# First norm's two chains in turn, the last stores on two queues, and C's transposes at later steps, in a two-layer hybrid trunk

## The chip, the cores and the metric

The kernel runs on one core of one Trainium2 chip. The metric is the device time of one execution in microseconds (us). Before the change the median of three runs is 414.24 us (413.98 to 414.63). All durations below come from one profiled execution of that kernel, which took 414.05 us.

## What is computed

The input x has 256 tokens of 1024 numbers. Two layers are applied, each h = h + Mixer(RMSNorm(h)), and a last RMSNorm. Layer 0 is a sparse attention mixer (compressed, selected and window branches, 16 heads, gated), layer 1 a diagonal state-space mixer (S5). The parts that matter here:

```python
def _rmsnorm(x, g):
    return x * rsqrt(mean(x * x, -1) + EPS) * g

# S5 parameters, from weights alone
dt  = exp(log_dt);  lre = minimum(lambda_re, -1e-4)
mag = exp(lre * dt); ab = mag * (cos(lim * dt), sin(lim * dt))
coef = (ab - 1) / lambda
bb  = coef * b                 # complex, 64 groups x 64 states x 16
y   = Re(c * scan(ab, bb * u)) + d_skip * u
```

The state-space layer's matrices (`ep` from C and the powers of ab, `bbn` from b and the powers) depend on weights alone, so they are computed in the background while the attention layer runs.

## The kernel before, in words

All work is on one core: 256 tokens are two halves of 128 (j = 0, 1), the 1024 model columns are eight slices of 128 (k). Weights stream from memory through four buffers `raw`, loaded by SyncE (SP, L193). A planner orders each engine's instructions by simulated times and by their order in the program; inside `tc.manual_schedule(engines=...)` the named engines keep the order of the program.

**The first norm (L326 to L352).** Each half of x (`xin`) is transposed by TensorE (L338) into PSUM banks `bts`. ScalarE squares a half and sums it on the way (L336), first half 0, then half 1. From each sum VectorE computes a reciprocal square root in one column per partition: `rsqrt_steps` (L283 to L302) is a start value and three rounds of two steps (L287, L290, then L297 and L299 three times). Six steps of the first chain run ahead, then the chains alternate (L340 to L343). `row_bcast` (L310) writes a diagonal matrix on VectorE into a piece of `xn`, and a matmul with ones makes `rb`, the factors as rows. After copies to `g0c` and `rrow`, eight operations (L350) write `xn`, the normed and transposed x. ScalarE then issues the loads of b and C (`s5_loads`, L175).

**What follows on TensorE.** `PRE` (L28) lists the first projections: `v0`, then `v1` with L875 ahead of it (the transpose of `rows`, a tile of small weights that SyncE loads at L355 to L362), `k0`, `k1`, `gt` (gates), `ck`, `cv`, `q0`. `v0` and `v1` run at L280, the others at L267. Each takes a PSUM bank of two that rotate; the gates take the bank of `k0` and so wait until VectorE has written `kl` (L795) from it. A matmul with f32 operands stands as two records in the trace.

**The parameter chain.** `chain_gen` (L394 to L480) is the computation of dt, mag, coef and ab on VectorE, some 100 small operations, which end in `nat2`. It is traced at L642 with a low priority, so the planner puts its steps into VectorE's gaps, also into those of the first norm.

**The background generator.** `s5_gen` (L484 to L640) does the rest in steps divided by `yield`. `adv(n)` takes n steps; hooks take one step (from `v1` on) or two (from `k1` on) with each weight tile of `PRE`, and the main loop over 24 attention units takes three a unit (`PACE`, L1132). The step numbers: 1 copies of b, 2 and 3 the transposes of `nat2` (L493) and VectorE's copies of them (L494), 3 to 6 the powers `pw` (L377), 7 to 9 the products for b (L534 to L538), 10 and 11 the transposes of C (L541 to L550), 12 to 14 the products for b2 (L551 to L555), then 24 `ep` products (L571 to L575) and 48 `bbn` products with their transposes (L597 to L604). All products are on GpSimd (POOL, L383). A transposed half of C goes through the one PSUM bank of the background to `c1c` and `c2c`, by ScalarE (L546, L548):

```python
for q in range(2):
    bt2 = bg_bank()
    for t in range(4):
        T.transpose(bt2[:, t * P:(t + 1) * P], cnat[:, 4 * q + t]..., ident)
    ...
    yield
```

**The bias of the compressed branch.** GpSimd writes `cbias` at the start of the program's attention part, with four operations (L672 twice, L675 twice).

**The end (L1447 to L1510).** The last projection gives five pieces of the output; for each VectorE adds the residual (L1451), ScalarE squares and sums (L1452), and GpSimd multiplies with the norm's weights (L1455, not for piece 4). `finish(j, i)` computes the factor of a half and scales: half 0 on ScalarE (L1461), then four stores on SyncE (L1463); half 1 on ScalarE (columns 0 to 511, L1465) and VectorE (768 to 1023 at L1466, 512 to 767 at L1467), then four stores of the left half on SyncE (L1469) and four of the right half, on ScalarE's queue and SyncE in turn (L1471).

Of the kernel before, what the change touches and what calls it, by code (L numbers as in the profile page):

```python
# [8 lines left out]
F32 = mybir.dt.float32  # L9
# [7 lines left out]
P = 128  # L17
# [29 lines left out]
def kernel(  # L47
# [132 lines left out]

    hooks = []
# [143 lines left out]

    xn = actp.tile([P, KT, S], F32, tag="actT", name="xn")  # L326
    sqs = xn.rearrange("p (j k) s -> p j (k s)", j=NQ)
    bts = [bank().rearrange("p (k s) -> p k s", k=2) for _ in range(KT // 2)]
    rb, gb0 = bank(), bank()
    rrow = const.tile([P, S], F32, name="rrow")  # L330
    E_ = mybir.EngineType
    with tc.manual_schedule(engines={E_.DVE, E_.Pool, E_.Activation}):
        sums, ys = [], [[], []]
        for j in range(NQ):
            sums.append(smp.tile([P, 1], F32, tag="ss", name="ss"))
            A.activation(sqs[:, j], xin[:, j], AF.Square, accum_out=sums[j])  # L336
            for k in range(KT):
                T.transpose(bts[k // 2][:, k % 2, j * P:(j + 1) * P], xin[:, j, k * P:(k + 1) * P], ident)  # L338
        rq = [rsqrt_steps(sums[j], ys[j]) for j in range(NQ)]
        for _ in range(6):  # L340
            next(rq[0])
        for r in (rq[1], rq[0]) * 12:
            next(r, None)  # L343
        for j in range(NQ):
            row_bcast(*ys[j], rb[:, j * P:(j + 1) * P], sqs[:, j, 0:P])
        T.transpose(gb0[:, :KT], nrow, ident[:KT, :KT])
        V.tensor_copy(g0c, gb0[:, :KT])
        V.tensor_copy(rrow, rb[:, :S])
        for k in range(KT):
            V.scalar_tensor_tensor(xn[:, k], bts[k // 2][:, k % 2], g0c[:, k:k + 1], rrow,  # L350
                                   op0=ALU.mult, op1=ALU.mult)
        s5_loads()  # L352

    rows = const.tile([56, P], F32, name="rows")
    nc.sync.dma_start(rows[8:24], pe_k.rearrange("(k l) d -> k (l d)", l=2))  # L355
    nc.sync.dma_start(rows[24:40], pe_v.rearrange("(k l) d -> k (l d)", l=2))
    nc.sync.dma_start(rows[0:8], n1.rearrange("(k p) -> k p", p=P))
# [3 lines left out]
    for u in range(2):  # L361
        nc.sync.dma_start(r4[:, u], d4[1 - u])  # L362
# [279 lines left out]
    with tc.high_priority(-CHOFF):  # L642
        for _ in chain_gen():
            pass
# [895 lines left out]
```

## Time and profile before

| | us |
|---|---|
| median of three runs | 414.24 (413.98 to 414.63) |
| the profiled execution | 414.05 |
| its span, first to last instruction | 412.3 |
| TensorE (PE) busy | 354.2 (86%) |
| GpSimd (POOL) busy | 269.3 (65%) |
| VectorE (DVE) busy | 227.9 (55%) |
| ScalarE (ACT) busy | 178.4 (43%) |
| bytes moved | 52.03 MB, mean 126 GB/s |

The execution's time is 1.75 us longer than its span. A busy TensorE is not TensorE at its peak: its matmuls are pipelined, and its granted clock has two levels, shown as 1.00 (2.4 GHz) and 0.50 (1.2 GHz). The mean granted clock of the execution is 0.933. Idle time of an engine costs something only where the chain of waits passes through it.

### The profile page before, as it was taken

To read this page: it belongs to the slowest core of one execution; us is meant where nothing else is said; L and a number is where in the kernel's file an instruction comes from. 1 tells how busy PE (TensorE), PEld (TensorE's weight loads), DVE (VectorE), ACT (ScalarE), POOL (GpSimd) and SP (SyncE) were. 2 spreads that over 40 slices of the span, in tenths; PEclk is the share of its full clock that TensorE was granted. 3 is DMA by queue.
4 is the path that set the end of the run, shared out by engine and by line. 5 is a ranking of instruction groups with operands and counts; after the bars stand their busy time and mean duration, and the time that the engine had idled before them with its cause. 6 is when DMAs were issued, how large, how long until landed. Compare 5 with 4: busy or idle time off the path is not lost.

```text
span 412.3 us, 6834 instructions
## 1 busy us (share of the span) xinstructions
PE 354.2 (86%) x2505; PEld 293.0 (71%) x2505; DVE 227.9 (55%) x582; ACT 178.4 (43%) x397; POOL 269.3 (65%) x281
## 2 busy tenths in 40 slices
PE   3899599999999998968998879994858599999990
PEld 3688468865888787644766657783847599999890
DVE  4969904433355243524555498563999944264243
ACT  3212420145366467566784454342513335444432
POOL 7009459989987789999544489321872476665760
PEclk9699979999999999985999999998696899999996
DMA  8964315558633315411311335996741215655403
GB/s 256 158 172 114 110 53 153 152 190 244 181 103 99 106 57 178 126 52 51 103 36 58 113 103 99 172 87 180 251 156 54 71 34 158 199 163 200 152 2 102
DMA packets 59970, 52.03 MB, mean 126 GB/s; under 512 B 21928, under 2 KB 52704, under 8 KB 59872
## 3 DMA queue, kind: packets, MB, share of 16 engines
q1 hardware_dynamic: 49536, 50.41, 43.9%
q10 hardware_dynamic: 10400, 1.18, 2.2%
q8 instruction: 20, 0.33, 0.4%
q14 instruction: 14, 0.11, 0.1%
HBM read 48.17 MB, written 1.05 MB: 119 GB/s over the span
## 4 chain that ended last, share of the span: by engine, by line
PE 57%; DVE 16%; SPq 6%; POOL 6%; DMA 5%; issue 5%; ACT 3%; DVEq 0%; ACTq 0%; POOLq 0%
PE b L267 16%; SPq L1181 5%; PE b L280 4%; PE b L224 4%; PE b L225 4%; PE b L226 4%; PE ob L986 3%; PE tu L973 2%; PE b L246 2%; PE b L244 2%; PE b L245 2%; DVE pw L377 2%; POOL wl L209 2%; PE cm L745 2%; DVE bbT L1357 2%
## 5 line engine op out<-in xcount | busy, mean ns | idle before, releaser
L209 POOL TENSOR_TENSOR wl<-raw,wh 128x1024 fp32r<-128x1024 f32 x30 | 74.3, 2480 | 48.3 <-ACT wh L207 48.1
L267 PE MATMUL b<-xn,raw 128*128 128x256 f32 (+1 forms) x400 | 94.9, 390 | 4.7 <-DVE kl L795 3.4
L267 PEld LDWEIGHTS b<-xn,raw 128*128 128x128 f32 (+1 forms) x400 | 74.1, 190 | 18.6 <-issue 4.6
L207 ACT ACTIVATE wh<-raw 128x1024 fp32r<-128x1024 f32 x48 | 50.8, 1058 | 67.0 <-PE b L225 20.7
L209 DVE TENSOR_TENSOR wl<-raw,wh 128x1024 fp32r<-128x1024 f32 x18 | 26.3, 1462 | 26.3 <-ACT wh L207 26.3
L959 ACT ACTIVATE pt<-pt,nm 128x128 f32<-128x128 f32 (+1 forms) x64 | 28.3, 444 | 24.8 <-DVE nm L955 24.7
L225 PE MATMUL b<-yl,wh 128*128 128x256 f32 x128 | 36.1, 283 | 0.0
L224 PE MATMUL b<-yh,wh 128*128 128x256 f32 x128 | 36.1, 284 | 0.0
L226 PE MATMUL b<-yh,wl 128*128 128x256 f32 x128 | 36.0, 283 | 0.0
L975 DVE COPY pT<-tu 128x512 f32<-128x512 f32 x24 | 16.6, 691 | 25.4 <-PE tu L973 24.7
L968 ACT ACTIVATE pt<-pt,su 128x128 f32<-128x128 f32 (+1 forms) x64 | 24.6, 443 | 11.6 <-DVE su L966 11.5
L224 PE MATMUL b<-xp,wh 128*128 128x256 f32 x64 | 20.2, 317 | 5.7 <-ACT wh L207 5.7
L224 PEld LDWEIGHTS b<-yh,wh 128*128 128x128 f32 x128 | 24.5, 192 | 0.2 <-issue 0.2
L225 PEld LDWEIGHTS b<-yl,wh 128*128 128x128 f32 x128 | 24.6, 192 | 0.0
L226 PEld LDWEIGHTS b<-yh,wl 128*128 128x128 f32 x128 | 24.5, 192 | 0.0
L383 POOL TENSOR_TENSOR ep<-c1c,pw 128x1024 f32<-128x1024 f32 x8 | 16.0, 2022 | 10.3 <-ACT c1c L546 5.3
L955 DVE CUSTOM_DVE_ANT_0 pt<-su,b 128x128 f32<-128x128 f32 (+1 forms) x64 | 19.4, 351 | 4.7 <-PE su L943 4.7
L226 PE MATMUL b<-xp,wl 128*128 128x256 f32 x64 | 20.1, 316 | 1.6 <-POOL wl L209 1.6
L383 POOL TENSOR_TENSOR bbn<-bbn,bbt 128x512 f32<-128x512 f32 x16 | 20.4, 1274 | 0.6
L383 POOL TENSOR_TENSOR bbn<-b1c,h 128x512 f32<-128x512 f32 x16 | 17.8, 1111 | 4.6 <-PE bg L604 4.4
L986 PE MATMUL ob<-pT,vsw 128*64 128x128 f32 x192 | 17.4, 297 | 3.4 <-DVE pT L975 3.4
L225 PE MATMUL b<-xp,wh 128*128 128x256 f32 x64 | 19.8, 311 | 0.0
(319 smaller groups left out, 874.1 us busy)
## 6 DMA issues: line engine op xcount, KB each, us to landing
raw<-in_l_w_in_dram SPq DMA_DIRECT2D x44, 512.0 KB, 4.0
raw<-in_l_w_out_dram SPq DMA_DIRECT2D x16, 512.0 KB, 3.9
raw<-in_l_w_glu_dram SPq DMA_DIRECT2D x16, 512.0 KB, 3.6
raw<-in_l_cmp_k_w_dram SPq DMA_DIRECT2D x4, 512.0 KB, 3.9
raw<-in_l_cmp_v_w_dram SPq DMA_DIRECT2D x4, 512.0 KB, 3.9
xin<-in_x_dram SPq DMA_DIRECT2D x2, 512.0 KB
h<-in_x_dram SPq DMA_DIRECT2D x8, 128.0 KB, 3.3
tm<-kt__2197 SPq DMA_DIRECT2D x4, 128.0 KB
```

What stands on the lines that cost most here:

```text
L207: A.activation(hi, raw, AF.Copy)
L209: lo_eng[-1].tensor_tensor(lo, raw, hi.bitcast(F32), op=ALU.subtract)
L224: T.matmul(dst, a, xh[:, k], start=(k == 0 and e == 0), stop=False)
L225: T.matmul(dst, a, xl[:, k], start=False, stop=False)
L226: T.matmul(dst, b, xh[:, k], start=False, stop=(k == KT - 1 and e == len(dsts) - 1))
L267: T.matmul(dst, w[:, i, e * m:(e + 1) * m], xn[:, k], start=(k == 0 and e == 0), stop=(k == KT - 1 and e == len(dsts) - 1))
L383: PL.tensor_tensor(o, a, b_, op=op)
L955: V.tensor_tensor_reduce(o.rearrange("p t k -> p (t k)"), sb[:, i * w + br * nk:i * w + (br + 1) * nk], self.b8[hf][:, S - nk:S], -0.125, ...
L959: A.activation(o, o, AF.Exp, scale=-1.0, bias=self.nm[:, j, hf, br:br + 1], accum_out=self.su[:, j, hf, br:br + 1])
L968: A.activation(o, o, AF.Copy, scale=r)
L986: T.matmul(self.ob[64 * hf:64 * hf + 64, j * P:(j + 1) * P], vsw[:, kt, br, 64 * g:64 * g + 64], p_, start=first, stop=last, tile_position ...
L1181: nc.sync.dma_start(tm[16 * s_:16 * s_ + 16, 16 * j:16 * j + 16].rearrange("p q l c -> p q (l c)")[:, :, 16 * l_:P], kt_[32 * j:32 * j + 1 ...
```

## The change

Four edits:

- The first norm. The second half's sum is computed on VectorE by `tensor_tensor_reduce`; the two chains take their steps in turn from the start; the diagonals are written into a piece of `cbias` instead of `xn`, for which the pool `att` and the tile `cbias` are opened before the norm; the transpose of the norm's weights moves ahead of the chains.
- The parameter chain. `chain_gen` (and the small helpers with it) is defined ahead of the norm, and its first three steps (23 operations on VectorE) stand in the manual order, behind `xn`. The rest is traced where it was.
- The transposes of C. One empty step ahead of the first half and two ahead of the second: steps 10 and 11 become 11 and 14, and everything behind them in the generator comes three steps later.
- The end. Piece 3 has no product on GpSimd; VectorE scales columns 512 to 1023 of half 1 in one operation; half 1 is stored in four whole rows, three from ScalarE's queue and one from SyncE.

```diff
+    att = tc.tile_pool(name="att", bufs=1, reuse_waits="tile")
+    atp = att.__enter__()
+    cbias = atp.tile([P, NQ, 16, NB], F32, name="cbias")
...
     with tc.manual_schedule(engines={E_.DVE, E_.Pool, E_.Activation}):
-        sums, ys = [], [[], []]
+        sums, ys = smp.tile([P, NQ], F32, name="ss0"), [[], []]
+        A.activation(sqs[:, 0], xin[:, 0], AF.Square, accum_out=sums[:, 0:1])
+        V.tensor_tensor_reduce(sqs[:, 1], xin[:, 1], xin[:, 1], 1.0, 0.0, ALU.mult, ALU.add, sums[:, 1:2])
         for j in range(NQ):
-            sums.append(smp.tile([P, 1], F32, tag="ss", name="ss"))
-            A.activation(sqs[:, j], xin[:, j], AF.Square, accum_out=sums[j])
             for k in range(KT):
                 T.transpose(bts[k // 2][:, k % 2, j * P:(j + 1) * P], xin[:, j, k * P:(k + 1) * P], ident)
-        rq = [rsqrt_steps(sums[j], ys[j]) for j in range(NQ)]
-        for _ in range(6):
-            next(rq[0])
-        for r in (rq[1], rq[0]) * 12:
+        rq = [rsqrt_steps(sums[:, j:j + 1], ys[j]) for j in range(NQ)]
+        T.transpose(gb0[:, :KT], nrow, ident[:KT, :KT])
+        for r in rq * 12:
             next(r, None)
         for j in range(NQ):
-            row_bcast(*ys[j], rb[:, j * P:(j + 1) * P], sqs[:, j, 0:P])
-        T.transpose(gb0[:, :KT], nrow, ident[:KT, :KT])
+            row_bcast(*ys[j], rb[:, j * P:(j + 1) * P], cbias[:, j, 0:8].rearrange("p h n -> p (h n)"))
         V.tensor_copy(g0c, gb0[:, :KT])
         V.tensor_copy(rrow, rb[:, :S])
         for k in range(KT):
             V.scalar_tensor_tensor(xn[:, k], bts[k // 2][:, k % 2], g0c[:, k:k + 1], rrow,
                                    op0=ALU.mult, op1=ALU.mult)
         s5_loads()
+        chain = chain_gen()
+        for _ in range(3):
+            next(chain)
...
+        yield
         for q in range(2):
+            if q:
+                yield
+                yield
             bt2 = bg_bank()
...
     with tc.high_priority(-CHOFF):
-        for _ in chain_gen():
+        for _ in chain:
             pass
...
-        if i == 4:
+        if i >= 3:
             return
         PL.tensor_tensor(hg[j][:, c0:c1], h1s[j][:, c0:c1], gf[:, c0:c1], op=ALU.mult)
...
         A.activation(ho[1][:, 0:512], hg[1][:, 0:512], AF.Copy, scale=y)
-        V.scalar_tensor_tensor(ho[1][:, 768:D], h1s[1][:, 768:D], y, gf[:, 768:D], op0=ALU.mult, op1=ALU.mult)
-        V.tensor_scalar(ho[1][:, 512:768], hg[1][:, 512:768], y, None, op0=ALU.mult)
+        V.scalar_tensor_tensor(ho[1][:, 512:D], h1s[1][:, 512:D], y, gf[:, 512:D], op0=ALU.mult, op1=ALU.mult)
         for l_ in range(4):
-            nc.sync.dma_start(o3[1, l_, :, 0:512], ho[1][32 * l_:32 * l_ + 32, 0:512])
-        for l_ in range(4):
-            (nc.scalar, nc.sync)[l_ % 2].dma_start(o3[1, l_, :, 512:D], ho[1][32 * l_:32 * l_ + 32, 512:D])
+            (nc.sync if l_ == 1 else nc.scalar).dma_start(o3[1, l_], ho[1][32 * l_:32 * l_ + 32])
```

## Rows read from the trace of the kernel before

**Rows 1.** Chain of waits of the whole span, shares by engine.
```profile
PE 57%; DVE 16%; SPq 6%; POOL 6%; DMA 5%; issue 5%; ACT 3%; DVEq 0%; ACTq 0%; POOLq 0%
```

**Rows 2.** Timeline of VectorE, first norm: start us, us, engine, line, operation.
```profile
6.10 0.81 DVE L299 SCALAR_TENSOR_TENSOR rs_y<-rs_t,rs_i 128x1 f32<-128x1 f32 x1
...
7.94 0.14 DVE L287 TENSOR_SCALAR rs_v<-ss 128x1 f32<-128x1 f32 x1
...
10.43 0.27 DVE L312 TENSOR_SCALAR xn<-ident,rs_y 128x128 f32<-128x128 f32 x1
...
11.68 0.53 DVE L419 RECIPROCAL den<-den 64x64 f32<-64x64 f32 x1
...
12.15 3.21 DVE L350 SCALAR_TENSOR_TENSOR xn<-b,g0c,rrow 128x256 f32<-128x256 f32 x8
```

**Rows 3.** Timeline of GpSimd, first 31 us; in brackets idle time before and releaser.
```profile
6.28 1.19 POOL L672 TENSOR_TENSOR cbias<-cdist,slopes 128x256 f32<-128x256 f32 x2
...
30.48 2.00 POOL L383 TENSOR_TENSOR b1c<-ep,pT 128x1024 f32<-128x1024 f32 x1 [22.10 <-DVE pT L494]
```

**Rows 4.** Timeline of TensorE, first projection; window by stage, its PEclk column is granted clock.
```profile
13.11 10.00 PE L280 MATMUL b<-raw,xn 128*128 128x256 f32 x32 [1.81 <-issue]
...
13.11:18.90 5.79, 5.79 (x14) 4.62 (x15) 5.55 (x32) 1.05 (x1) 0.00 (x0) 0.50 0.96 150
```

**Rows 5.** Timelines of TensorE and VectorE, 46 to 59 us.
```profile
46.49 0.66 PE L544 MATMUL bg<-ident,ep 128*128 128x128 f32 x4 [1.16 <-DVE pT L494]
50.58 8.45 PE L267 MATMUL b<-xn,raw 128*48 128x256 f32 x24 [3.43 <-DVE kl L795]
...
48.60 3.48 DVE L795 TENSOR_TENSOR kl<-b,kh 64x256 fp32r<-64x256 f32 x8
```

**Rows 6.** Timelines of TensorE and ScalarE, 23 to 30 us.
```profile
23.24 6.31 PE L280 MATMUL b<-raw,xn 128*128 128x256 f32 x28
29.48 0.46 PE L493 MATMUL bg<-ident,nat 64*128 64x64 f32 x4
...
25.56 0.42 ACT L466 ACTIVATE nat<-nat 64x256 f32<-64x256 f32 x1 [1.81 <-DVE nat L377]
```

**Rows 7.** Timeline of GpSimd, 48 to 60 us; window by stage, fifth busy column is POOL.
```profile
48.62 5.97 POOL L383 TENSOR_TENSOR ep<-c1c,pw 128x1024 f32<-128x1024 f32 x3 [5.33 <-ACT c1c L546]
59.54 2.02 POOL L383 TENSOR_TENSOR ep<-c1c,pw 128x1024 f32<-128x1024 f32 x1 [4.96 <-PE bg L544]
...
87.00:150.00 63.00, 61.99 (x393) 49.82 (x392) 26.24 (x97) 33.70 (x107) 52.32 (x59) 1.00 0.50 148
```

**Rows 8.** Timelines of VectorE, GpSimd and SyncE, the end; window, last two columns DMA share, GB/s.
```profile
401.86 0.69 DVE L297 SCALAR_TENSOR_TENSOR rs_t<-rs_i,rs_v 128x1 f32<-128x1 f32 x1
...
405.50 0.48 DVE L1466 SCALAR_TENSOR_TENSOR tm<-h,rs_y,gf 128x256 f32<-128x256 f32 x1
...
400.55 1.99 POOL L1455 TENSOR_TENSOR tm<-h,gf 128x512 f32<-128x512 f32 x2 [3.66 <-DVE h L1451]
...
405.29 1.76 SPq L1463 DMA_DIRECT2D out_dram<-tm  x4
...
409.15 0.84 SPq L1471 DMA_DIRECT2D out_dram<-tm  x2
...
405.30:412.30 7.00, 0.00 (x0) 0.00 (x0) 0.91 (x3) 0.72 (x1) 0.00 (x0) 0.50 0.54 150
```

**Rows 9.** Groups by line and shape, VectorE's reduction: count, busy us, mean ns.
```profile
L955 DVE CUSTOM_DVE_ANT_0 pt<-su,b 128x256 f32<-128x256 f32 x32 | 12.1, 417 | 0.0
...
L955 DVE CUSTOM_DVE_ANT_0 pt<-su,b 128x128 f32<-128x128 f32 x32 | 7.3, 285 | 4.7 <-PE su L943 4.7
```

**Rows 10.** SyncE's timeline and waits; L875's instructions on TensorE (ns, first and last start).
```profile
18.41 1.56 SPq L362 DMA_DIRECT2D rows<-in_l_d_dram  x2
...
SPq L362 <- DMA ep<-in_l_b_im_dram: 1.0, 1, 1.0
...
L875 PEldq EVENT_SEMAPHORE  x3: 51/51/51, 21.3 to 21.6; - x3
```

More of the change, by code (lines that the diff above doesn't have):

```diff
@@ L480, in chain_gen @@
         yield
+    xn = actp.tile([P, KT, S], F32, tag="actT", name="xn")
+    sqs = xn.rearrange("p (j k) s -> p j (k s)", j=NQ)
+    bts = [bank().rearrange("p (k s) -> p k s", k=2) for _ in range(KT // 2)]
+    rb, gb0 = bank(), bank()
+    rrow = const.tile([P, S], F32, name="rrow")
+    E_ = mybir.EngineType
+    with tc.manual_schedule(engines={E_.DVE, E_.Pool, E_.Activation}):
+        sums, ys = smp.tile([P, NQ], F32, name="ss0"), [[], []]
+        A.activation(sqs[:, 0], xin[:, 0], AF.Square, accum_out=sums[:, 0:1])
+        V.tensor_tensor_reduce(sqs[:, 1], xin[:, 1], xin[:, 1], 1.0, 0.0, ALU.mult, ALU.add, sums[:, 1:2])
+        for j in range(NQ):
+            for k in range(KT):
+                T.transpose(bts[k // 2][:, k % 2, j * P:(j + 1) * P], xin[:, j, k * P:(k + 1) * P], ident)
+        rq = [rsqrt_steps(sums[:, j:j + 1], ys[j]) for j in range(NQ)]
+        T.transpose(gb0[:, :KT], nrow, ident[:KT, :KT])
+        for r in rq * 12:
+            next(r, None)
+        for j in range(NQ):
+            row_bcast(*ys[j], rb[:, j * P:(j + 1) * P], cbias[:, j, 0:8].rearrange("p h n -> p (h n)"))
+        V.tensor_copy(g0c, gb0[:, :KT])
+        V.tensor_copy(rrow, rb[:, :S])
+        for k in range(KT):
+            V.scalar_tensor_tensor(xn[:, k], bts[k // 2][:, k % 2], g0c[:, k:k + 1], rrow,
+                                   op0=ALU.mult, op1=ALU.mult)
+        s5_loads()
+        chain = chain_gen()
+        for _ in range(3):
+            next(chain)
+    rows = const.tile([56, P], F32, name="rows")
+    nc.sync.dma_start(rows[8:24], pe_k.rearrange("(k l) d -> k (l d)", l=2))
+    nc.sync.dma_start(rows[24:40], pe_v.rearrange("(k l) d -> k (l d)", l=2))
+    nc.sync.dma_start(rows[0:8], n1.rearrange("(k p) -> k p", p=P))
+    nc.sync.dma_start(rows[40:48], d_skip.rearrange("(k g) c -> k (g c)", k=8))
+    d4 = d_skip.rearrange("(k j u) c -> u k j c", k=8, j=4)
+    r4 = rows[48:56].rearrange("k (j u c) -> k u j c", j=4, u=2)
+    for u in range(2):
+        nc.sync.dma_start(r4[:, u], d4[1 - u])
+    colsT = const.tile([P, 56], F32, name="colsT")
+    bbT.insert(0, (0, actp.tile([P, NB0, P], F32, tag="actT", name="bbT0")))
     sh_ld = {}
@@ L650, in adv @@
                 next(bg, None)
-    att = tc.tile_pool(name="att", bufs=1, reuse_waits="tile")
-    atp = att.__enter__()
     dist = atp.tile([P, S], F32, name="dist")
@@ L666 @@
     PL.tensor_scalar(cdist, cdist, -15.5, None, op0=ALU.add)
-    cbias = atp.tile([P, NQ, 16, NB], F32, name="cbias")
     slopes = atp.tile([P, 16], F32, name="slopes")
```

29 lines of the change are left out of this document (removed).

## Prediction

> **What bounds the kernel now.** First the chain of waits: TensorE has 57% of it and VectorE 16% [rows 1], so an edit counts where the chain leaves TensorE. The change touches three such places, and I read the timelines there.
>
> The first is the start. VectorE's timeline [rows 2] shows the first norm's two chains of one-column steps: a step that takes 0.14 to 0.22 us undisturbed took 0.81 at 6.10, ending as the first of GpSimd's two cbias products ends [rows 3]. So the second chain begins only at 7.94, though its sum is there at 6.9; its diagonal is written at 10.43 behind parameter steps of `chain_gen`, and a reciprocal at 11.68 stands between the copy of `rrow` and the first `xn` at 12.15. TensorE starts L280 at 13.11, just after the second `xn`, takes 10.0 us for its first 32 records, and runs at the granted clock of 0.50, the lower level (1.2 GHz), until 18.9 [rows 4].
>
> The second is 45 to 50 us. The transposes of C (L544) run at 46.49 inside a gap of TensorE, and the gate matmuls start at 50.58, when VectorE has written the first four of eight `kl` pieces [rows 5]. Those 24 matmul records took 0.35 us each, against 0.225 for the 28 at 23.24 [rows 6]: the gap costs clock too. GpSimd starts its `ep` products at 48.62, right after C is evicted, does three and waits 4.96 us for the second half [rows 7].
>
> The third is the end. The last matmul ends at 401.1, but SyncE issues ten stores one after the other from 405.29 to 409.99, and the span ends at 412.3 [rows 8].
>
> **The change part by part.**
>
> *Second sum on VectorE.* `tensor_tensor_reduce` has no row at 1024 columns. Two forms of the same line give 0.285 us at 128 and 0.417 at 256 [rows 9], or 1.03 ns a column: 1.21 us plus 0.08 for the read. x's second half lands at about 5.7, so both sums stand at 7.05. Bounds: 4 x 0.417 = 1.7 us, if nothing in it is fixed, and about 1.0. GpSimd still clears `kl` until 6.28; the one-column steps beside that clearing were not stretched, so I add nothing.
>
> *Chains in turn.* `cbias` is now the scratch for the diagonals, so GpSimd's four cbias operations (2.1 us) have to wait for the diagonal matmuls, until about 10.1. Behind them in GpSimd's queue stands nothing due before 30.48, where GpSimd had been idle for 22.1 us [rows 3]: that wait costs nothing. Beside `xn` they cost nothing either, if `xn` (one operand from PSUM) behaves like `kl`, whose eight pieces, also from PSUM, kept 0.42 us each beside GpSimd's `ep` products [rows 5, 7]; if not, they hold `xn` for 2 us. The second chain alone went from 7.94 to its last step at 9.62, 1.7 us; the two in turn fit each into the other's pauses, so the second diagonal is written at 7.05 + 1.7 + 0.2 = 8.95, not 10.43. Without the parameter steps and the reciprocal (0.53) `xn` starts 1.55 us behind that diagonal (now 1.72, of which the steps in between give back a part), at 10.5 instead of 12.15: L280 starts at 11.45, 1.65 us sooner.
>
> *The cover that goes.* After 32 records L280 hands over to L875, the transpose of `rows`. The last of those loads is issued at 19.3 (two in 1.56 from 18.41), since SyncE waits there for the landing of b_im, which this change only asks for a little sooner; TensorE's sequencer took its semaphores at 21.3 to 21.6 [rows 10]. Now that hides under L280, which ends at 23.11. With L280 1.65 sooner it ends at 21.45 at the old clock, or near 18.5 at the full one: both ways L875 waits for `rows`, and the next matmuls begin at about 21.4 instead of 23.24. I take -1.8 us. Bounds: 0, if `rows` lands as late as 23.05 would still allow, and the step after it.
>
> *Parameter chain.* Its first 23 steps now stand behind `xn`, in order. By the pace of such steps (0.18 us, the reciprocal 0.53) they end at 17.9, some 0.75 later than now. ScalarE's copy of the first parameters, now at 25.56 for 0.42 us, ends at 26.8, and the transposes at 29.48 need it [rows 6]. At 29.48 - 1.8 = 27.7 it is still hidden; it caps the gain at 2.7 us. From there to 50.58 the run goes through VectorE and `kl`, and carries the -1.8 along.
>
> *C one step later, two apart.* Removed from the gap: four transposes, which hid there for nothing, since the gates wait for `kl` anyway. They go behind the gate matmuls, onto TensorE's line: 0.44 to 0.66 us, the pace of L544's two groups; I take +0.45. ScalarE's three evictions follow them. GpSimd is queued behind those: 50.58 - 1.8, plus 16 gate records at 0.35 (5.6), plus transposes and eviction (1.2) starts `ep` at 55.6 instead of 48.62. Three products of 2 us without a stall bring its fourth to 61.6, where it now is at 59.54: 2 us late, or 4 against TensorE. Between 87 and 150 us GpSimd is idle for 63.0 - 52.3 = 10.7 us [rows 7], which takes that up. I take +0.3; bounds 0 and +6, the three products in full.
>
> *End.* Piece 3 loses its GpSimd product. VectorE's step at 401.86 took 0.69, ending as GpSimd ends at 402.54; at 0.22 the whole chain to the scale of the second half is 0.47 sooner. One `scalar_tensor_tensor` of 512 columns replaces 256 + 256: 0.48 at 256 [rows 8], about 0.75 at 512, the same end as now, 405.8. Stores: SyncE issues five and ScalarE three at 0.43, so the last issue ends at 407.15, not 409.99. By the issues alone that is -2.85, less 0.4 because the pieces are twice as large: -2.4. But the transfers were busy for 0.54 of 7.0 us, 3.8 us at full share, and cannot begin before 405.3: they end at 409.1, at best, where they now end near 410.85. That makes -1.75, and it is the nearer of the two; without the 0.47 and with a slow first microsecond it is -1.1.
>
> On that the Trainium skill, page DMA: Bandwidth & Descriptors, section Issuing engines are not separate DMA queues, says that transfers from several issuing engines share the same 16 DMA engines, and a second issuer saves issue time only. By it alone the gain could be read as small; the trace disagrees in so far as 4.7 us of issues end the kernel here, against 3.8 us of transfers. By the rule's limit the sum has -1.75, by the issues -2.4.
>
> **Sum:** -1.8 + 0.45 + 0.3 - 1.75 = -2.8 us. The profiled execution took 414.05 us, of which 412.3 is the span; it lies 0.19 under the median of the runs, 414.24. That gives 411.25, or 411.4 on the median: I say 411.3.
>
> **The rivals.**
>
> (A) *Only the end pays.* `rows`, or GpSimd's holding `xn`, gives the start back, and the C transposes cost their 0.45: +0.45 - 1.75 = -1.3, 412.8. For it: the loads of `rows` keep their place on SyncE. Against it: the sequencer's 21.3 to 21.6.
>
> (B) *The clock holds.* TensorE's gap before L280 shrinks from 5.1 to 3.4 us and the clock fell at 12.1, after the new start. If it stays at 2.4 GHz, or comes back sooner at both places, and `rows` is also earlier, the cap of 2.7 is reached and up to 0.8 of the gate matmuls' slow time goes: -2.7 - 0.8 + 0.45 - 1.75 = -4.8, 409.3. The Trainium skill, TensorE: Matmul & The Clock Gate, Part 1, says that a long idle time brings the half rate back and activity lifts it; no run here shows it yet for a gap as short as that.
>
> (C) *GpSimd becomes the bound: slower.* From 158 to 182 us the chain runs through GpSimd. If its idle time before is not free for the late `ep` work, because what fills it stands behind TensorE's steps, the 6 us arrive there: -1.8 + 0.45 + 6.0 - 1.75 = +2.9, 417.0. It decides from 3.1 us of late work on the chain, where -1.8 + 0.45 - 1.75 is used up. Against it: 10.7 idle microseconds.
>
> (D) *The stores do not gain, the start little*: the transfers or their receipts end the kernel as now. -0.9 + 0.45 + 0.3 - 0.3 = -0.45, 413.6.
>
> **How the numbers follow.** Chances: forecast 0.5, A 0.17, B 0.15, C 0.1, D 0.08. About 0.2% (0.83 us) is what a measurement of this kernel can tell from no change. Forecast, A and B lie below 413.4: faster 0.82. D and the near side of C lie within: 0.09. The rest of C is slower: 0.09. The range reaches from 408.9, just past B, to 413.2, past A; it leaves out most of C and D, and the far end of B.
>
> **What would show it.** At the start: no one-column step above 0.3 us, the cbias products behind 10 us, `xn` at 10.5, L280 at 11.4, and L875 waiting for `rows`; L280's next group at 21.4. In the middle: gates at 48.8, L544 behind them, `ep` from 55 to 56 without a stall of 5 us, and the last `bbn` on GpSimd no later than at 198. At the end: the step after `rs_i` at 0.22, the last store issued 2.8 us sooner, the span's end 1.7 sooner against the last matmul. The forecast is wrong if L875 doesn't wait, if TensorE's gates do not follow `xn`, or if GpSimd's chain between 158 and 182 grows.

## The result, and the profile after

The changed kernel takes 419.26 us (median of six runs, 417.58 to 424.0) against 413.4 for the kernel before (six runs, 412.34 to 414.63). Medians and ranges are of all runs; the ratios, here and below, leave out runs more than 1.5% above the fastest of the same kernel (here the 424.0, in e2 three of six, in e4 one, in e6 two). The ratio is 1.0129, 95% interval 1.0095 to 1.0163: slower by 5.3 us. The forecast was 411.3, with a range from 408.9 to 413.2; the result lies outside it, on the other side, and also beyond the 417.0 of rival C. The profiled execution took 419.07 us with a span of 417.4. Its chain of waits by engine, which answers to [rows 1]:

```profile
PE 64%; DVE 17%; DMA 7%; issue 4%; ACT 3%; POOL 3%; SPq 0%; DVEq 0%; ACTq 0%; POOLq 0%
```

TensorE holds more of it. SyncE's issues, 6% before, are gone, but most of that share was not the stores of the end: 5% were SyncE's issues of the transfers into `tm` at L1181, from 262 to 282 us, which the change does not touch (3% in e3, 4% in e17).

The start came as forecast. VectorE's timeline of the changed kernel answers to [rows 2]:

```profile
5.83 1.22 DVE L454 CUSTOM_DVE_ANT_0 xn<-xin 128x1024 f32<-128x1024 f32 x1 [3.38 <-DMA xin<-in_x_dram]
...
8.72 0.48 DVE L317 TENSOR_SCALAR cbias<-ident,rs_y 128x128 f32<-128x128 f32 x2
...
10.26 3.23 DVE L467 SCALAR_TENSOR_TENSOR xn<-b,g0c,rrow 128x256 f32<-128x256 f32 x8
```

The sum on VectorE takes 1.22 us, the diagonals are written at 8.72, `xn` begins at 10.26 (forecast 10.5). GpSimd's `cbias` operations ran beside it from 9.70, and eight pieces in 3.23 us show that they did not hold it. TensorE's timeline is where the plan breaks; it answers to [rows 4 to 6] (L285 was L280, L882 was L875, L499 was L493, L554 was L544, L272 was L267):

```profile
11.42 8.83 PE L285 MATMUL b<-raw,xn 128*128 128x256 f32 x32 [1.66 <-DVE xn L467]
21.80 0.24 PE L882 MATMUL cm<-ident,rows 56*128 56x56 f32 x1 [1.55 <-DMA rows<-in_l_d_dram]
21.97 7.17 PE L285 MATMUL b<-raw,xn 128*128 128x256 f32 x32
28.98 1.89 PE L272 MATMUL b<-xn,raw 128*128 128x256 f32 x8
30.80 0.46 PE L499 MATMUL bg<-ident,nat 64*128 64x64 f32 x4
...
47.81 1.11 PE L554 MATMUL bg<-ident,ep 128*128 128x128 f32 x4 [3.74 <-DVE pT L500]
51.89 9.50 PE L272 MATMUL b<-xn,raw 128*48 128x256 f32 x32 [2.97 <-DVE kl L802]
61.23 0.27 PE L554 MATMUL bg<-ident,ep 128*128 128x128 f32 x1
```

L285 starts at 11.42 (forecast 11.45), L882 waits for `rows`, and the next group begins at 21.97 instead of 23.24. Up to here TensorE is 1.27 us ahead. But the transposes of `nat2` (L499) now stand behind all 32 records of that group and 8 of `k0`, where they stood behind 28 of it: 30.80 instead of 29.48, although ScalarE has the first part of `nat2` ready at 25.86 + 0.42 = 26.28 (its timeline):

```profile
25.86 0.42 ACT L428 ACTIVATE nat<-nat 64x256 f32<-64x256 f32 x1 [4.97 <-DVE nat L339]
```

From there everything on the way to the gates is 1.3 us late, and they start at 51.89 instead of 50.58. Of C, only the second half moved in TensorE's order. The first still runs in the gap; the second, which in TensorE's timeline before stood in one piece behind the gate matmuls,

```profile
58.86 0.60 PE L544 MATMUL bg<-ident,ep 128*128 128x128 f32 x4
```

goes one transpose at a time between later matmuls from 61.23. GpSimd's timeline shows the wait for it (answers to [rows 7]):

```profile
49.84 6.01 POOL L345 TENSOR_TENSOR ep<-c1c,pw 128x1024 f32<-128x1024 f32 x3 [5.23 <-ACT c1c L556]
64.09 2.03 POOL L345 TENSOR_TENSOR ep<-c1c,pw 128x1024 f32<-128x1024 f32 x1 [8.24 <-PE bg L554]
```

The fourth product starts 4.55 us later than before. That shows up much later. The instructions of the tile `bbn` on GpSimd from 192 us on (count, ns, first to last start), before:

```profile
L383 POOL TENSOR_TENSOR bbn<-bbn,bbt x2: 1267/1272/1277, 192.8 to 196.9; 128x512 f32<-128x512 f32 x2
```

and after, with one more of the 16 sums left to do, and the last 10.2 us later:

```profile
L345 POOL TENSOR_TENSOR bbn<-bbn,bbt x3: 1265/1272/1281, 199.0 to 207.1; 128x512 f32<-128x512 f32 x3
```

In the last attention units TensorE then waits for GpSimd, and its clock falls a second time. Its waits in the kernel before, from 183 us to the end of the units at 224.2 (us in all, times, longest):

```profile
PE ob L986 <- DVE pT L975: 3.4, 5, 0.8
PE su L942 <- DVE nm L955: 1.6, 1, 1.6
PE tu L973 <- ACT pt L968: 1.5, 1, 1.5
```

and the window of the same stretch (behind its length the busy time of PE, PEld, DVE, ACT and POOL, then granted clock, DMA share, GB/s):

```profile
183.00:224.20 41.20, 34.83 (x221) 23.84 (x222) 19.97 (x81) 28.89 (x90) 25.05 (x45) 0.84 0.17 52
```

The changed kernel's waits from 183 us to the end of its units at 229.9, and its window:

```profile
PE b L251 <- POOL ozl L1046: 2.6, 1, 2.6
PE tu L980 <- ACT pt L975: 2.0, 2, 1.2
PE bg L614 <- POOL bbn L345: 2.0, 3, 0.8
PE ob L993 <- DVE pT L982: 1.9, 3, 0.8
PE su L949 <- DVE nm L962: 0.4, 1, 0.4
```

```profile
183.00:229.90 46.90, 40.26 (x227) 26.17 (x228) 20.18 (x81) 29.70 (x91) 28.32 (x48) 0.82 0.16 46
```

The waits alone do not make the loss. Of the 4.6 us for GpSimd in the second list, the 2.6 for `ozl` ended at 183.26 and so lie almost wholly ahead of the window; before, TensorE waited 1.47 and 0.52 us in the same place, until 182.1. The later waits for `bbn` are 0.83 us at 204.99 and 0.53 at 208.38. TensorE's idle time is nearly the same in the two windows (41.20 - 34.83 = 6.37 us and 46.90 - 40.26 = 6.64); its busy time is up by 5.4 us, with six records more. The windows around the two waits, before and then after, show what else differs:

```profile
203.00:208.00 5.00, 4.22 (x35) 3.03 (x33) 3.29 (x12) 3.53 (x12) 1.89 (x7) 1.00 0.00 0
208.00:213.00 5.00, 4.22 (x27) 2.91 (x28) 2.09 (x13) 4.46 (x13) 1.99 (x4) 1.00 0.00 0
```

```profile
203.00:208.00 5.00, 2.75 (x13) 1.51 (x12) 1.27 (x8) 3.53 (x14) 4.67 (x9) 0.86 0.01 4
208.00:213.00 5.00, 4.62 (x26) 3.96 (x26) 2.37 (x8) 3.53 (x11) 1.35 (x4) 0.50 0.77 206
```

TensorE is busy for only 2.75 us of the first five, and then its granted clock is 0.50, the lower level, where before it stayed at 1.00. (The first fall, at about 183 us, is in both kernels.) The units fall behind here: the 56th of the `tu` transposes starts 1.1 us later than before (187.05 against 185.93), and the units end 5.7 us later. How the 4.5 us added in between divide among the waits, the order of the work and the clock is not shown. The second layer from there takes 187.5 us instead of 188.1.

The end, timelines of VectorE, SyncE and ScalarE, which answer to [rows 8]:

```profile
411.34 0.75 DVE L1473 SCALAR_TENSOR_TENSOR tm<-h,rs_y,gf 128x512 f32<-128x512 f32 x1
...
411.12 1.76 SPq L1470 DMA_DIRECT2D out_dram<-tm  x4
412.99 0.36 SPq L1475 DMA_DIRECT2D out_dram<-tm  x1
...
412.18 1.32 ACTq L1475 DMA_DIRECT2D out_dram<-tm  x3
```

The last issue ends at 413.50, 2.2 us behind the start of the scaling (before 4.5), and the span ends 6.06 us behind the start of the scaling instead of 6.8. From the end of the last matmul to the end of the span it is 8.88 us instead of 9.93.

### The profile page after: what moved, and what is told of

Same layout as the page of the kernel before. It is cut to its first block, busy times and chain, and to the rows that moved or that the text cites. A ratio compares the mean times of both kernels' runs of the same rounds, so it can differ in the third digit from the quotient of the medians.

```text
span 417.4 us, 6833 instructions
## 1 busy us (share of the span) xinstructions
PE 357.8 (86%) x2505; PEld 294.4 (71%) x2505; DVE 224.8 (54%) x583; ACT 177.0 (42%) x395; POOL 268.1 (64%) x280
## 4 chain that ended last, share of the span: by engine, by line
PE 64%; DVE 17%; DMA 7%; issue 4%; ACT 3%; POOL 3%; SPq 0%; DVEq 0%; ACTq 0%; POOLq 0%
PE b L272 18%; PE b L229 4%; PE b L230 4%; PE b L231 4%; PE b L249 4%; PE b L250 3%; PE ob L993 3%; PE tu L980 3%; DMA ep<-in_l_b_im_dram 3%; PE b L251 3%; DVE pw L339 2%; PE bg L614 2%; PE b L285 2%; PE cm L752 2%; DVE bbT L1364 2%
## 5 line engine op out<-in xcount | busy, mean ns | idle before, releaser
L272 PE MATMUL b<-xn,raw 128*128 128x256 f32 (+1 forms) x400 | 94.5, 388 | 4.7 <-DVE kl L802 3.0
L272 PEld LDWEIGHTS b<-xn,raw 128*128 128x128 f32 (+1 forms) x400 | 73.7, 190 | 18.8 <-issue 3.8
L229 PE MATMUL b<-xp,wh 128*128 128x256 f32 x64 | 19.9, 312 | 4.3 <-ACT wh L212 4.3
L980 PE MATMUL tu<-ident,pt 128*128 128x128 f32 x96 | 19.2, 312 | 2.1 <-ACT pt L975 2.0
```

The lines of the kernel that those rows point to most:

```text
L229: T.matmul(dst, a, xh[:, k], start=(k == 0 and e == 0), stop=False)
L272: T.matmul(dst, w[:, i, e * m:(e + 1) * m], xn[:, k], start=(k == 0 and e == 0), stop=(k == KT - 1 and e == len(dsts) - 1))
L980: T.transpose(tb[:, i * P:(i + 1) * P], self.pt[u][:, i], ident)
```

## The experiments

"Gates" is the start of the first gate matmul; "units done" is the start of GpSimd's clearing of `tm`, which waits for the last attention unit. These two columns are of the profiled run.

| kernel | median us (range) | gates, us | units done, us | ratio to before (95%) |
|---|---|---|---|---|
| before | 413.4 (412.34 to 414.63) | 50.58 | 224.20 | 1 |
| changed | 419.26 (417.58 to 424.0) | 51.89 | 229.86 | 1.0129 (1.0095 to 1.0163) |
| e1 C alone | 416.36 (415.54 to 418.34) | 50.38 | 228.37 | 1.0064 (1.0041 to 1.0086) |
| e2 start alone | 423.19 (417.32 to 425.8) | 52.00 | 226.76 | 1.016 (1.0112 to 1.0209) |
| e3 end alone | 412.46 (410.66 to 413.73) | 50.19 | 223.74 | 0.9959 (0.9942 to 0.9976) |
| e4 start, end | 417.97 (415.71 to 423.65) | 51.89 | 226.78 | 1.0096 (1.0061 to 1.013) |
| e5 norm, end | 419.75 (418.5 to 422.97) | 55.20 | 230.76 | 1.0159 (1.0106 to 1.0211) |
| e6 parameter steps alone | 416.57 (414.5 to 422.8) | 58.12 | 231.53 | 1.0077 (1.0043 to 1.0111) |
| e7 end, three steps behind C | 411.9 (410.36 to 413.86) | 50.02 | 223.06 | 0.9959 (0.9931 to 0.9987) |
| e8 end, C one later | 412.43 (410.69 to 413.51) | 49.77 | 222.59 | 0.9963 (0.9937 to 0.9989) |
| e9 end, copies on ScalarE | 413.42 (411.82 to 414.27) | 51.90 | 225.43 | 1.0 (0.998 to 1.0019) |
| e10 start, end, copies on ScalarE | 415.45 (413.74 to 418.07) | 51.09 | 225.96 | 1.0078 (1.0049 to 1.0108) |
| e11 end, products held | 415.35 (412.67 to 417.83) | 47.58 | 229.08 | 1.007 (1.0046 to 1.0094) |
| e12 start, end, products held | 420.31 (419.25 to 421.7) | 48.47 | 229.74 | 1.0181 (1.0154 to 1.0208) |
| e13 as e4, ep waits for copies | 416.72 (415.0 to 419.2) | 51.61 | 226.16 | 1.0086 (1.0053 to 1.0119) |
| e14 as e4, nat2 placed | 413.74 (411.78 to 415.97) | 49.23 | 224.04 | 1.0017 (0.9995 to 1.0039) |
| e15 changed, ep waits for copies | 418.87 (417.86 to 423.38) | 53.07 | 232.23 | 1.0156 (1.0115 to 1.0197) |
| e16 start alone, one more run | 417.46 | 51.15 | 227.31 | |
| e17 changed, nat2 placed | 416.36 (415.2 to 419.84) | 49.86 | 227.34 | 1.0078 (1.0052 to 1.0104) |
| e18 as e14, rows later | 412.42 (409.54 to 413.87) | 48.27 | 223.05 | 0.9968 (0.9944 to 0.9992) |

**e1 to e4: one part at a time.** e1 puts only this into the kernel before; e4 takes it out of the changed one:

```diff
+        yield
         for q in range(2):
+            if q:
+                yield
+                yield
             bt2 = bg_bank()
```

> The kernel before with only the three empty steps around the transposes of C. Theory (late background): TensorE has the background's last transposes (of bbn) in its queue one attention unit later and waits for GpSimd there, at 180 to 210 us; this alone makes the loss: +5 to +7 us against the kernel before, the last bbn on GpSimd at 205 to 209 us instead of 197, and the transposes of nat2 at 29.5 us as in the kernel before. Rival (late parameter chain): the loss comes from the transposes of nat2, which the changed start put 1.3 us later; then this kernel is within +1 us. Rival (clock): the slow clock at 183 to 196 us makes the loss, and it differs from run to run of one schedule; then the profile has +5 us with no wait of TensorE for GpSimd.

e2 has only the first two edits of the change, e3 only the last.

> The kernel before with only the changed first norm and the first 23 parameter steps in the manual order. Theory (late background): the 1.25 us that TensorE gains up to 21.8 us are given back where the transposes of nat2 stand 6 matmuls later in its queue; gates at 51.5 to 52 us, total within 0.8 us of the kernel before. Rival (late parameter chain): +3 to +6 us, seen as later ep and bbn products on GpSimd up to the end of the attention units. Rival (the start pays, C alone took it away): -1.2 to -1.8 us.

> The kernel before with only the changed end (no GpSimd product for piece 3, one scaling of 512 columns, four whole rows stored from two queues). Forecast of the prediction: -1.75 us (bounds -1.1 and -2.4). Theory from the changed kernel's trace, where the stretch from the scaling to the end took 6.06 us instead of 6.8: -0.7 for the stores and up to -0.5 for the product, so -0.7 to -1.2 us. Rival (the stores gain nothing): within 0.3 us.

> The changed kernel with the transposes of C at their old steps (the three empty steps taken out). Theory (late background): all of the loss is gone and the end's gain is left, -0.7 to -1.5 us against the kernel before, the last bbn on GpSimd at 196 to 199 us. Rival (late parameter chain): still +2 to +5 us. Rival (start pays): -2.5 to -3 us.

Measured: C alone costs 0.64%, 2.6 us, not the 5 to 7 that the theory gave it; its last `bbn` sum starts at 204.9, as late as the theory said, and GpSimd's stall for the second half is 8.8 us (the waits of tile `ep` in e1):

```profile
  PE bg L548: 8.8, 1
```

The end alone gains 0.41% (1.7 us, 1.0 to 2.4). That is the prediction's figure, but the interval also holds the upper part of the 0.7 to 1.2 that one trace had suggested, and the traces stay with about 1.2: from the end of the last matmul to the end of the span it is 8.71 to 8.94 us in the fifteen profiles with the changed end, and 9.93 to 10.18 in the five with the old one. The start alone, expected within 0.8 us, is slower, and so is e4 (+0.96%). So "late background" explains half at most: the start is no gain given back, but a loss. It also spreads the runs over 8 us (e2: 417.32 to 425.8).

**e5 to e8: which part of the start, which part of C.** e5 takes the 23 parameter steps out of the manual order, e6 puts only them in:

```diff
-        chain = chain_gen()
-        for _ in range(3):
-            next(chain)
...
-        for _ in chain:
+        for _ in chain_gen():
             pass
```

> The changed first norm and the changed end, with the parameter chain traced wholly at its old place and the transposes of C at their old steps. Theory (late parameter chain): the 23 steps in the manual order are what put the transposes of nat2 six matmuls later in TensorE's queue; without them they stand where they stood, at about 28 to 28.5 us instead of 30.8, the gates follow at 49.3, and the start pays: -1.2 to -1.6 us besides the end's -1.5, -2.5 to -3.2 us in all, with no run above 414 us. Rival (the norm itself, by TensorE's earlier start or its other clock, makes the loss of the start): +2 us or more, as with both.

> The kernel before with only the first 23 parameter steps in the manual order behind xn; norm, transposes of C and end as before. Theory (late parameter chain): the transposes of nat2 stand six matmuls later, at 31.5 to 32.5 us instead of 29.5, and nothing pays for it: +3 to +9 us, with runs far apart and a lower mean clock in the long ones. Rival (the norm itself makes the loss): within 0.8 us of the kernel before.

e6 agrees with the theory in the place (nat2's transposes at 31.49) and in the sign: +0.77%, runs from 414.5 to 422.8. e5 does not: it was to gain 2.5 to 3.2 us and lost 6.6. Its VectorE timeline shows why:

```profile
10.53 0.15 DVE L336 TENSOR_SCALAR xd<-ldt 64x1 f32<-64x1 f32 x1 [2.10 <-DMA ldt<-in_l_log_dt_dram]
```

With the norm earlier, the planner put the first parameter step into the norm's chain, and there VectorE stood 2.1 us for the load of log_dt. The manual steps behind `xn` protect against that; taking them out swaps one delay for another, so the time of e5 doesn't tell the two theories apart. Its order does: without the manual steps the transposes of `nat2` stand behind 30 records of `v1`, where they stood behind 28, and not behind 32 and 8 of `k0`. So the steps are what moves them. Both e5 and e6 show something else. The gates of e6 start only at 58.12, and `kl` at 56.14, because the last four copies of powers into `pws` (tile h) took 6.15 us together. The copies' line in e6 from 49 us on (count, shortest, median and longest in ns, first and last start):

```profile
L536 DVE COPY h<-pw x4: 227/2054/2058, 50.1 to 54.2; 128x128 f32<-128x128 f32 x4
```

GpSimd and VectorE beside and behind them, in e6's timelines:

```profile
50.15 5.98 POOL L341 TENSOR_TENSOR ep<-c1c,pw 128x1024 f32<-128x1024 f32 x3 [4.84 <-DVE pw L335]
...
56.14 3.48 DVE L799 TENSOR_TENSOR kl<-b,kh 64x256 fp32r<-64x256 f32 x8
```

and the same copies in the kernel before:

```profile
L532 DVE COPY h<-pw x4: 219/220/226, 48.1 to 48.5; 128x128 f32<-128x128 f32 x4
```

A copy of 0.22 us takes 2.05, the length of one `ep` product, when it meets one: three of the four in e6, two in e5. The Trainium skill, page SBUF — State Buffer, section SBUF: two separate sides, says that VectorE and GpSimd share one pair of ports under an exclusive lock, held for the whole instruction by whichever starts first, in some kinds of VectorE operations. The trace agrees for these copies; `kl`, with an operand from PSUM, keeps 0.43 us a piece beside the same products. In the kernel before the last copy starts at 48.5 and `ep` at 48.62 [rows 7]: the margin is a tenth of a microsecond.

> The changed end, and three empty steps in the background generator, behind the transposes of C instead of ahead of them and between them. Theory (C's place): only the transposes' place behind the gate matmuls costs, since GpSimd then waits 8 us for the second half; this kernel has no such wait and is within 0.5 us of the kernel with the changed end alone. Rival (number of steps): everything behind comes three steps later all the same, so +2 to +3 us against the kernel with the changed end alone, +0.5 to +1.5 against the kernel before.

```diff
             yield
+        yield
+        yield
+        yield
         ptt(b2c, bb, gb(crs))
```

> The changed end, and the transposes of C one step later but not two steps apart. Theory (two apart): the empty steps between the halves make C's whole cost, so this is within 0.5 us of the kernel with the changed end alone. Rival (one later): half of C's +2.7 us or more is here, +1.3 us against the kernel with the changed end alone.

e7 and e8 are the end alone again (0.9959 and 0.9963). Three steps later cost nothing, one step later costs nothing. By exclusion the two empty steps between the halves, which leave GpSimd waiting for the second half behind its first three products, make C's loss; no run has these two steps alone.

**e9 to e12: is it VectorE's chain from pT to kl?** e9 and e10 move the eight copies to ScalarE; e11 and e12 hold GpSimd's six products for b back until the powers are there:

```diff
-            V.tensor_copy(pws[:, :, s_], pw[:, :, 8 - l_])
+            A.activation(pws[:, :, s_], pw[:, :, 8 - l_], AF.Copy)
...
+        PL.tensor_copy(b1v[:, 0, 0:1], pr[:, 8, 0:1])
         ptt(b1v, ba, gb(pT[:, 2]))
```

(the same line ahead of the products into `tb_` and `b2c`).

> The changed end, and the eight copies of the powers into pws on ScalarE instead of VectorE. Theory (VectorE's chain from nat2 to kl, stretched by GpSimd): between 30 and 50 us VectorE runs without a pause from pT through the powers to kl, and the gate matmuls wait for kl. Without the copies kl starts about 1.1 us sooner (seven copies at 0.22, less waits that pass on to the next step), gates at 49.1 instead of 50.2: -0.5 to -1.2 us against the kernel with the changed end alone, -2.2 to -2.9 against the kernel before, and runs no further apart than 3 us. Rival (clock): nothing at the gates decides, so no change against the changed end alone.

> The changed first norm with its 23 parameter steps, the changed end, C as before, and the copies into pws on ScalarE. Theory (the last copies against GpSimd's first ep product): in the runs far above the others the last four copies fall beside ep and take up to 6 us instead of 0.63, as in the profile of the kernel with the parameter steps alone; with the copies off VectorE no run can fall into that: all runs within 3 us of each other, the median 414 to 415.5, no run above 417. Rival (clock): a lower clock falls on single runs whatever VectorE does; runs still from 415 to 424.

> The changed end, and GpSimd's six products for b held back (by a one-column copy of the last power into each target) until VectorE has the powers. Theory (stretched chain): the 13 small steps of VectorE that took 1.8 to 2.4 us beside these products take 0.2 to 0.4; the powers are ready near 38 instead of 48 us, kl then waits for ScalarE's kh or TensorE's k0, gates at 47.5 to 48.5 instead of 50.2: -1.5 to -2.7 us against the kernel with the changed end alone. Rival (GpSimd is the bound): the products end at 50 us instead of 43.3, ep comes later and the end of the attention units with it: 0 to +3 us against the changed end alone.

> The changed first norm with its parameter steps, the changed end, C as before, and GpSimd's six products for b held back until VectorE has the powers. Theory (stretched chain): VectorE no longer sets the gates, so the later place of the transposes of nat2 costs nothing and TensorE's start reaches the gates: k0 is done near 44 us, gates at 46 to 47.5; -3 to -4.5 us against the kernel with the changed end alone, 408 to 410 us. Rival (GpSimd is the bound): 413 us or more. Rival (late nat2 decides by something else than kl): no better than the same hold without the changed start.

e10 is the only one that comes near what was expected: its median of 415.45 is inside, and the runs lie closer than e4's, though two are above 417. e12 is furthest off (gates at 48.47, 1.81% slower). In e9 `kl` then waits for ScalarE (3.27 us for `kh`), and the gates come later, at 51.90. e11 does what its edit says: the last power starts at 37.4, the gates at 47.58 (TensorE's timeline):

```profile
47.58 5.55 PE L267 MATMUL b<-xn,raw 128*48 128x256 f32 x24 [1.13 <-DVE kl L798]
```

and nothing comes of it. The eleventh record of the tile `ob`, at 113.14 us before, starts at 106.19, 7 us sooner; the units are done at 229.08, 5 us later. Gates 3.0 us sooner, kernel 0.7% slower. So the time of the gates alone decides nothing when TensorE's order behind them has changed too, as the traces of e11 and e3 show it has.

**e13 to e16: the two causes apart.** e13 and e15 make the first `ep` product wait for the copies, with one small copy from `pws` into its target. e14 writes TensorE's order through `v1` and `k0` by hand, so that the `nat2` transposes stand behind 30 and 41 matmuls (counted from `v0` on, two records each), as before:

```diff
+            if q == 0:
+                PL.tensor_copy(ep[:, 0, 0, 0:8], pws[:, 0, :, 0])
             ptt(ep[:, gs], c1c[:, gs].unsqueeze(2).to_broadcast(sh), pe_(0))
```

```diff
+        if i in (1, 2):
+            if i == 1:
+                pe_order = tc.manual_schedule(engines={mybir.EngineType.PE})
+                pe_order.__enter__()
+            mid.append({1: 6, 2: 9}[i])
+            while name not in done:
+                step(name)
...
```

> The changed start and end, C as before, and GpSimd's first ep product made to wait for VectorE's copies into pws (an eight-column copy from pws into its target, which the product overwrites). Theory (a lost race: the last four copies take 0.63 us when they end before ep starts, up to 6.2 us when they don't): the long runs go; all runs within 3 us, none above 418, median 415 to 416.5, where the same kernel without the wait had 415.7 to 423.65. Rival (clock): runs still up to 421 or more.

> The changed start and end, C as before, and TensorE's order written out by hand through the two projections v1 and k0, so that the transposes of nat2 stand behind 30 and 41 matmuls as in the kernel before. Theory (the place of nat2's transposes gives the start back): they run at 28.0 to 28.5 us, pT at 28.7, gates at 49.0 to 49.5; the fastest runs 1 us under those of the changed end alone, 410 to 411.5, though some runs may still lose the race of the copies. Rival (the start's loss comes from later, the order of the attention units): 415 us or more with gates at 49.

> The changed kernel, with GpSimd's first ep product made to wait for the copies into pws. Theory (late nat2 and late C cost 5 us in every run, the lost race comes on top in single runs): no run above 420.5, median 417 to 419. Rival (the race is the loss in most runs): median 414 to 416. Rival (clock): as without the wait, up to 424.

> The changed start alone, for a second profile. Theory (lost race): if the run is long (421 to 426 us), the last copies into pws take 3 to 6.2 us, kl starts at 53 to 56 us and the gates at 55 to 58 us; if it is short (417 us), they take 0.63 and the gates start at 52. Rival (clock): a long run with the gates at 52 and more time at the lower clock from 180 us on.

e14 settles the place of nat2's transposes. Its TensorE timeline:

```profile
28.13 0.46 PE L506 MATMUL bg<-ident,nat 64*128 64x64 f32 x4
...
49.23 3.19 PE L276 MATMUL b<-xn,raw 128*48 128x256 f32 x7 [3.43 <-DVE kl L805]
```

With nothing but the order of these matmuls changed against e4, the gates start 2.66 us sooner, the units are done 2.74 sooner, and the ratio falls from 1.0096 to 1.0017. In between the lead stays at 2.65 to 2.80 us, and from the 53rd `tu` transpose on TensorE's order (tile and shape of every record) is the same in both traces, so it is the place that makes the difference.

e14 does not reach e3, though at the 56th `tu` transpose it is 1.0 us ahead of it (184.60 against 185.58), as at the gates. From there to the end of the units e14 takes 39.44 us and e3 38.16. The kernels whose TensorE order from the 53rd `tu` on is e14's, e2, e4 and e18, take 39.36 to 39.42; those with e3's order, the kernel before and e9, 38.27 and 38.26. So the lead goes in the other order that the planner wrote for the last units when the start changed. e5, e10, e13 and e16 have e14's order too and take 40.4 to 40.7; in their traces the granted clock falls to 0.50 a second time in the last units, between 215 and 221 us. e16 is the same kernel as e2, so this fall comes in one execution and not in another; the stretch takes 40.63 us with it and 39.36 without. In the four kernels with late C (changed, e1, e15, e17) the second fall comes at 204 to 210 us in every profile, and the stretch takes 42.1 to 43.1 us; in the kernel before, e3, e7, e8 and e9, with C early and the old start, there is none.

The wait in e13 narrows the runs (415.0 to 419.2), though not to the 3 us expected; the intervals of its ratio and of e4's overlap, and e15 still has runs up to 423.38. So the lost race is shown in the two profiles of e5 and e6, and not shown to be what makes long runs of the changed kernel; e16 gave a short run (417.46, copies 0.63). One thing that varies between the profiles is seen in the TensorE timeline of e15, a run of 421.05:

```profile
22.94 0.24 PE L884 MATMUL cm<-ident,rows 56*128 56x56 f32 x1 [2.94 <-DMA rows<-in_l_d_dram]
```

Here TensorE waits 2.94 us for `rows`, 1.55 in the changed kernel, 1.51 in e13, 0.43 in e4, and not at all in e14 and e16: a load's landing, which before was covered, can now set TensorE's time.

**e17 and e18.** e17 is the changed kernel with e14's order; e18 is e14 with the transpose of `rows` moved:

```diff
         if i == 1:
-            b = bank("cm", 1)
-            T.transpose(b[:, :56], rows, ident[:56, :56])
-            V.tensor_copy(colsT, b[:, :56])
             hooks.append(lambda: adv(1))
         if i == 3:
+            b = bank("cm", 1)
+            T.transpose(b[:, :56], rows, ident[:56, :56])
+            V.tensor_copy(colsT, b[:, :56])
             hooks.append(lambda: adv(1))
```

> The changed kernel with the transposes of nat2 back behind 30 and 41 matmuls; C stays at its later steps. Theory (place of nat2's transposes, worth 2.6 us at the gates and 4.2 in the medians with C as before): gates at 49.3 instead of 51.9, median 414.5 to 416.5 instead of 419.3; what is left above the kernel before is C's. Rival (C's late half decides alone in the last attention units): 418 us or more.

> The changed start and end, nat2's transposes behind 30 and 41 matmuls, and the transpose of rows behind the 30th matmul, where no load is waited for. Theory (uncovered wait): v1 follows v0 at 20.2 us instead of 21.7, nat2's transposes run at 26.8 to 27.2, gates at 47.8 to 48.2; the runs lie no further apart than 2.5 us and the median is 411.5 to 412.8. Rival (the order of the last attention units gives any gain back): 413.5 us or more with the gates at 48.

e17 is at 416.36, 2.9 us under the changed kernel in the medians (0.51% in the ratios, 2.1 us), with the gates at 49.86. What is left above e14, 0.61% or 2.5 us, is C's, the same as in e1. e18 has the gates at 48.27 and beats the kernel before by 0.32% (0.08 to 0.56), e14 by 2.0 us in the ratios and by 1.0 in the two profiles, at the gates and at the end of the units. In e14's profile TensorE did not wait for `rows`, so the pair does not show what that wait is worth. Its TensorE timeline at the start:

```profile
11.55 15.62 PE L292 MATMUL b<-raw,xn 128*128 128x256 f32 x60 [1.63 <-DVE xn L474]
27.11 0.27 PE L887 MATMUL cm<-ident,rows 56*128 56x56 f32 x1
```

Sixty records run through without a wait. Its spread, 4.3 us, stayed. It is no better than e3, e7 and e8, which leave the start alone: these four beat both kernels, and three of them have the end without the rest.

## Why the prediction was wrong

**The sum in measured terms** (ratios times 413.5): end -1.7; C +2.6; nat2's place +2.1 (changed kernel) to +3.3 (e14 against e4); the rest of the start +2.4 (e14 against e3), of which e18 gets 2.0 back. That is +5.4 to +6.6, measured +5.3; each ratio is good to about 0.2 to 0.3%, 1 us or so. The forecast had -1.75, +0.75 for C with GpSimd's delay, and -1.8.

**Start: right to 21.8 us, wrong behind it.** `xn`, L280 and the wait for `rows` came within 0.3 us, the next group 0.6 late. The step that failed is the sentence "At 29.48 - 1.8 = 27.7 it is still hidden", with "carries the -1.8 along": it took the transposes of `nat2` for work that follows its data. They are work at a fixed place in TensorE's queue, and the planner chose a new place, six matmuls later, when 23 steps ahead of them moved into a fixed order. The data was there at 26.28; the queue was not. e14 shows what it costs, since it moves the place alone, and e5 and e6 show that the steps move it. The change names the steps that move; what else the planner moves has to be asked of every engine's order.

**The clock of rival B** came in part: from 12 to 20 us the granted clock is 0.79 instead of 0.57, TensorE having begun before it fell, and the first 32 records take 8.83 us instead of 10.00. L882's wait for `rows` swallows that.

**The cover that goes** was seen, but priced as a cap on the gain. It also ties TensorE to a landing for which it waited between nothing and 2.94 us in the profiles with the new start.

**C: wrong in place and price.** "They go behind the gate matmuls" failed: the first half stayed in the gap (47.81), and the second, behind the gates already before (58.86), went further back. GpSimd's delay of 4.55 us was inside the bound of +6, but "which takes that up" failed: the idle time of 87 to 150 us was no reserve. In the changed kernel GpSimd is busy for 53.7 us of that stretch, 1.4 more than before, and yet writes 15 pieces of `bbn` there instead of 17. The largest part of its idle time, 4.4 us of 10.7 before and 3.0 of 9.3 after, is the wait for TensorE's transposes of the previous `bbn`, so a late GpSimd doesn't catch up by itself there. Late work then arrives in the last units, as rival C said, though with 2.6 us rather than 6, and with a cost for which the prediction had no term: behind the late `bbn` the clock of TensorE falls a second time. C named the point from which it decides, 3.1 us of lateness on the chain; the rest of the loss had another source, so C's 417.0 came near for a partly wrong reason.

**The end** met its figure partly by luck: -1.7 in the runs (1.0 to 2.4) against -1.75, but about -1.2 in the traces, near the prediction's lower bound of -1.1. The 0.47 us of the chain came as 0.31 (from the end of the last matmul to the start of the scaling, 3.13 before and 2.82 in e3). By the issues alone it would have been -2.4; the sum by the time that the transfers need was the nearer. In e3's trace the last issue ends 2.16 us behind the start of the scaling, where before it was 4.49, but the span ends 3.82 us behind that issue instead of 2.31. The Trainium skill, page DMA: Bandwidth & Descriptors, section Issuing engines are not separate DMA queues, says that a second issuing engine saves issue time only, since all transfers run on the same DMA engines. The trace agrees: 2.3 us of issues were saved, and 1.5 of them were lost again in the landing. The last matmul, which the prediction has end at 401.1, ends at 402.37; its sum does not use that time.

**What stays open:** why the other order of TensorE makes the last units 1.2 us longer (no run pins that order to the old one); how far the second fall of the clock and the waits ahead of it each make C's cost; and what makes single runs of the kernels with the new start up to 8 us longer. In the longest runs of e2 and e4 the mean granted clock is 0.917 to 0.922, in their shortest 0.935 and 0.937, but whether the clock is the cause or follows from other waits is not shown.

## What to carry to other kernels

A planner's order is part of the change: before a gain upstream is carried forward, compare each engine's order and ask where the next cross-engine step stands in the queue, not when its data is ready. Idle time of an engine is a reserve only if what ends it does not depend on that engine's own earlier work. An edit that starts work sooner may uncover the loads behind it; look at what waits for them as well. And read the granted clock behind a new wait: here 1.4 us of waits stand at the beginning of a stretch at the lower clock.

## What was unexpected of the hardware

A small VectorE copy beside a long GpSimd product does not slow down, it stops: 0.22 us became 2.05, the product's length, three times in a row in e6 and twice in e5 (4.31 us for the four copies), decided by a tenth of a microsecond between two engines. Eight stores of 128 KB from two queues took 3.1 and 2.7 us to land in the changed kernel, where before twelve (four of 128 KB, eight of 64) took 2.0 to 2.5; that took back more than half of what the issues gave. And the granted clock of TensorE fell a second time in the last units of one execution of a kernel and not of another: with the same order of TensorE the stretch took 40.63 us (e16) instead of 39.36 (e2).
